# Four plain output row tiles become two, with tables shared by three head pairs and transposes taken half by half

## The chip, the cores and the metric

The kernel runs on one core of one Trainium2 chip. The metric is device time of one execution in microseconds. Engines are called TensorE (PE in the profile, its weight loads PEld), VectorE (DVE), ScalarE (ACT), GpSimd (POOL) and SyncE (SP), whose queue issues nearly all DMA transfers.

## What is computed

One layer: RMS norm of x (2048 rows of 1024), one projection to q, k, v and a gate, neighbourhood attention on a grid of 32 x 64 tokens with 16 heads of 64, a gate by SiLU, the output projection, the residual, and a last RMS norm.

```python
h = rmsnorm(x, norm_0)
q, k, v, gate = split(h @ w_in, 4)            # each (2048, 1024), 16 heads
# token (r, c) attends to 8 rows x 16 columns around it, clipped at the edges of the grid
s = q @ k.T / 8 + rpb[head, row offset, column offset]
o = softmax(s) @ v
x = x + (o * silu(gate)) @ w_out
return rmsnorm(x, norm_f)
```

All is float32. A float32 product is made as three matmuls of split operands: each operand is split into a high part (a ScalarE copy) and the rest (a VectorE subtraction), and high x high, high x low and low x high are summed in PSUM.

## The kernel before

**Products.** A product of a 2 x 2 block matrix is made by seven block products instead of eight ("seven products", Winograd's form). The input projection is made so in stages one and two, but for three units of it (`halves`, L252 on, 288 matmuls of 128x512) that are left for the time of attention. The output projection has 16 row tiles of 128 rows. Row tiles 0 to 3 (`PLAIN = 4`, L33) are plain: 24 matmuls for each half of the columns, 48 a tile (`outputs`, L1550). The others go in pairs by seven products of 12 matmuls each, 84 a pair, behind attention (`rows_by_seven`, L1708; `PAIRS`, L1601).

**Attention** is 32 runs (`order`, L1214): a run is a head pair p (0 to 7) and a row block T (0 to 3). First come T = 1 and 0 of all head pairs, then T = 2 and 3. A run has two quads of 32 query columns each. One pass of the main loop (L1811) works on two runs at once; in the order of TensorE's instructions it is

1. the filling: a given number of plain matmuls (`amount[m]`, L1753), first the 288 of the projection, then the plain row tiles. Between them lie the scaling of the second quad's softmax weights for run m-1 (`normalise`, L1330: GpSimd, ScalarE and VectorE a part each) and one or two operations that split weights or row tiles (`consume`, `split_rows`),
2. `turns(m - 1)` (L1347): 48 transposes of the softmax weights X, 16 for each of three PSUM bank pairs `ph`, each pair copied to `pta` by ScalarE and VectorE,
3. `scores(2m)` and `scores(2m+1)` (L1298): 64 matmuls s; VectorE adds the bias table and takes the maximum (L1320), ScalarE the exponential (L1327). They write X, so they come after the transposes that read it,
4. `values(m - 1)` (L1371): 36 matmuls o, one VectorE product with the gate, and the store of the result to `ogd[T]` in DRAM.

The amounts are 13.5 matmuls in every run but the first two and the last. A run wants its k (`load_k`), q, values, gate and bias table (`load_bias`, L1260) loaded; the loads are put into SyncE's queue at due times counted in filling matmuls (`begin`, L1790; `later_loads`, L1782): gate 1, bias 3 and 4.5, values 4, q 7, k 12. What isn't due at the end of a run is issued at the start of the next. A table is one of three kinds: "mid", "top" (brought by T = 0) and "end" (brought by T = 3). The middle table of a head pair is loaded for T = 1 and again for T = 2.

**Row tiles.** `load_og` (L1414) loads the gated result of a row tile from `ogd[T]`, `split_og` (L1424) splits it, `load_res` (L1420) loads the residual x into one of three buffers, which the square of the row (L1463) frees; `add_rows` and `finish` (L1436, L1471) add, square, take the root, scale and store. The order of the plain half tiles is `turns_` (L1532). Row pairs load their parts with `load_rows_of` (L1637).

Of the kernel before, what the change touches and what calls it, by code (L numbers as in the profile page):

```python
# [11 lines left out]
F32 = mybir.dt.float32  # L12
# [12 lines left out]
NP = H // 2  # L25
# [4 lines left out]
NF_SCALE = -2 * ROOT[0] * 0.375 * ROOT_K ** 2  # L30
NEG = -1e30
RES_BUFS, RES_EARLY = 3, 1
PLAIN = 4  # L33

FRAME, TALL = [0, 4, 12, 17], 15
HALF_ROWS = [[(0, 8), (0, 11)], [(0, 11), (4, 11)], [(0, 11), (4, 11)], [(3, 11), (7, 8)]]
# [25 lines left out]
def build(ctx, tc, x, xr, xt, wg, bias, w_out, n0, nf, out):  # L62
    nc = tc.nc
# [3 lines left out]
    kd = [dram.tile([128, S], F32, name=f"kd{p}") for p in range(NP)]  # L67
    sgd = [dram.tile([128, S], F32, name=f"sgd{p}") for p in range(NP)]
    vd = [dram.tile([4, S, 128], F32, name=f"vd{u}") for u in range(2)]
    ogd = [dram.tile([128, 4, NP, 128], F32, name=f"ogd{T}") for T in range(4)]  # L70
    vsd = {f: dram.tile([4, 128, 512], F32, name=f"vsd{f}") for f in ("S1", "S4")}
    vsp = {f: dram.tile([4, 2, 128, 512], F32, name=f"vsp{f}") for f in ("S2", "S3")}
    vu1 = dram.tile([4, 128, 512], F32, name="vu1")
# [9 lines left out]
    raw = pool("raw", 6)  # L83
# [36 lines left out]
    def bank(n, name):  # L120
        return banks.tile([128, n], F32, name=name, tag="bank")
# [208 lines left out]
    def store(key, lag, f):  # L330
        n = len(later)
        while n and later[n - 1][0] > clock[0] + lag:
            n -= 1
        later.insert(n, (clock[0] + lag, key, f))
# [856 lines left out]
    def projections():  # L1191
        for n, (kind, j, ph, c) in enumerate(halves):
            state["half"] = n
            w = (KINDS[kind] + j, ph)
            for a in range(2):
                if n == len(halves) - 5 and a == 0:
                    for k in range(RES_EARLY):
                        load_res(*turns_[k])
                if n == len(halves) - 1:
                    if a == 0:  # L1200
                        store(("ogl",), 20, lambda: (load_og(0), load_og(1)))
                    else:
                        store(("og0",), 19, lambda: split_og(0))
                consume(1)
                p = yield from group(w, a, c, n)
                state["event"] = clock[0]
                give(kind, 2 * j + a, c, p, True)
            state["done_halves"] = n + 1
# [2 lines left out]

    KT, VT, QT, EM, SG = {}, {}, {}, {}, {}
    stored_at = {}
    order = [(p, T) for p in range(NP) for T in (1, 0)] + [(p, T) for p in range(NP - 2) for T in (2, 3)]  # L1214
    order += [(NP - 2, 2), (NP - 1, 2), (NP - 1, 3), (NP - 2, 3)]
    pairs = [(p, T, quad) for p, T in order for quad in range(2)]
    PARTS = {1: (4, 19, 8), 0: (0, 4, 0), 2: (12, 28, 0), 3: (28, 32, 0)}
# [1 line left out]
    def load_k(p, T):  # L1219
        r0, r1, more = PARTS[T]  # L1220
        base = 12 * (T > 1)
        a, b = r0 * GW, r1 * GW + more
        must(*[("k", p, c) for c in range(a // 512, (b + 511) // 512)])

        def keys():
            if T in (1, 2):
                khalf.clear()
                KT[p, T // 2] = (kp([128, 2048], F32, "kt") if p % 2 == 0 else mkp([128, 1536], F32, "kt"))[:, :1344]
            t = KT[p, T // 2]
            if T == 2:  # L1230
                nc.gpsimd.memset(t[:, 1280:1288], 0.0)
            nc.sync.dma_start(t[:, a - base * GW:b - base * GW], kd[p][:, a:b])

        return keys
# [22 lines left out]
    kinds_of = {0: ("top", "mid"), 1: ("mid", "mid"), 2: ("mid", "mid"), 3: ("mid", "end")}  # L1257
    BRINGS = {0: "top", 1: "mid", 2: "mid", 3: "end"}

    def load_bias(p, T):  # L1260
        fs = []
        kind = BRINGS[T]
        w = 2 * WIDE * TABLES[kind][2]
        EM[p, T // 2, kind] = []
        for quad in range(2):
            t = mp([128, 512], F32, "em")[:, :w]
            EM[p, T // 2, kind].append([t[:, :w // 2], t[:, w // 2:]])
            o = TABLE_AT[kind] + quad * w
            fs.append(lambda t=t, o=o, w=w: nc.sync.dma_start(t, bias[p, :, o:o + w]))
        return fs  # L1270
# [27 lines left out]
    def scores(i, between=None):  # L1298
        p, T, quad = pairs[i]
        kt, qt = KT[p, T // 2], QT[p, T]  # L1300
        both = [bank(512, f"s{s}") for s in range(2)]
        places = {}
        for half, (u, n) in enumerate(HALF_ROWS[T]):
            for s in range(2):
                places[half, s] = both[s][:, 256 * half:256 * half + WIDE * n]
            for h in range(4):
                g = 4 * quad + h
                for s in range(2):
                    a = slice(s * 64, s * 64 + 64)
                    o = (FRAME[T] + u - 12 * (T > 1)) * GW + 8 * FIRST[g]  # L1310
                    nc.tensor.matmul(places[half, s][h * 32:h * 32 + 32], qt[a, g * 64 + half * 32:g * 64 + half * 32 + 32],  # L1311
                                     kt[a, o:o + n * GW].rearrange("p (r c) -> p r c", c=GW)[:, :, :WIDE],
                                     start=True, stop=True, skip_group_check=True)
        ST[i] = st = tiny.tile([128, 12], F32, name="st")
        for half, (u, n) in enumerate(HALF_ROWS[T]):
            xs_ = [by_column(X[quad, half, s], HALF_ROWS[T][half]) for s in range(2)]
            table = EM[p, T // 2, kinds_of[T][half]][quad]
            for s in range(2):
                o = 2 * half + s
                nc.vector.tensor_tensor_reduce(xs_[s], places[half, s].rearrange("p (r c) -> p c r", c=WIDE),  # L1320
                                               table[s].rearrange("p (c r) -> p c r", c=WIDE), -1.0, 1e38,
                                               OP.add, OP.min, st[:, o:o + 1])
            if between and half == 0:
                between()
            for s in range(2):
                o = 2 * half + s
                nc.scalar.activation(xs_[s], xs_[s], AF.Exp, bias=st[:, o:o + 1], scale=-1.0,  # L1327
                                     accum_out=st[:, 4 + o:5 + o])
# [18 lines left out]
    def turns(m):  # L1347
        p, T = order[m]
        k = 8 * TALL
        PT[m] = pt([128, 3072], F32, "pta")  # L1350
        t = PT[m].rearrange("p (s b n c) -> p b s n c", s=2, b=3, c=64)
        for b in range(3):
            ph = [bank(512, f"ph{h}") for h in range(2)]
            at = (2 - b) * k
            for quad in range(2):
                for half in range(2):
                    for s in range(2):
                        for h in range(2):
                            q = slice(64 * h, 64 * h + 64)
                            o = s * 256 + half * 128 + quad * 64  # L1360
                            nc.tensor.transpose(ph[h][:k, o:o + 64], X[quad, half, s][q, at:at + k], ident[q, q])  # L1361
            for h in range(2):
                o, i_ = t[:k, b, :, h::2], ph[h][:k].rearrange("p (s n c) -> p s n c", s=2, c=64)
                if h:
                    nc.vector.tensor_copy(o, i_)  # L1365
                else:
                    nc.scalar.activation(o, i_, AF.Copy)  # L1367
        if m + 1 < cycles:
            clear_x(order[m + 1][1])

    def values(m):  # L1371
# [16 lines left out]
        nc.vector.tensor_tensor(og, o, SG.pop((p, T)), OP.mult)  # L1388

        def keep():  # L1390
            nc.sync.dma_start(ogd[T][:, :, p], og.rearrange("p (i q) -> p i q", i=4))
            written.add(("og", p, T))
            stored_at[p, T] = clock[0]

# [19 lines left out]
    def load_og(n):  # L1414
        T, i = divmod(n, 4)
        must(*[("og", p, T) for p in range(NP)])
        G[n] = t = wp([128, NK, 128], F32, "ograw")
        nc.sync.dma_start(t, ogd[T][:, i])

    def load_res(n, j):  # L1420
        RES[n, j] = rbp([128, 512], F32, "xr")
# [14 lines left out]
    def add_rows(n, j, ps):  # L1436
        xr = RES.pop((n, j))
        state["event"] = clock[0]
        if n not in Y:
            Y[n] = [None, None], tiny.tile([128, 8], F32, name="st3")  # L1440
        y, st = (raw if j and n < 1 else ev)([128, 512], F32, "y"), Y[n][1]
        Y[n][0][j] = y
        if n == tiles - 1:
            cut = [slice(0, 256), slice(256, 512)] if j else [slice(0, 512)]
# [84 lines left out]
            scale()  # L1529
            store(("y", n), 18, send)  # L1530

    turns_ = [(0, 0), (1, 0), (2, 0), (0, 1), (1, 1), (2, 1), (3, 0), (3, 1)]  # L1532
    place = {}
    for k, (n, j) in enumerate(turns_):
        place.setdefault(n, k)
# [101 lines left out]
    def load_rows_of(m, f, home=None):  # L1637
        n, half = PAIRS[m][int(f[1]) - 1], int(f[2]) - 1
        T, i = divmod(n, 4)
        must(*[("og", p, T) for p in range(NP) if p // 4 == half])  # L1640
        A[m, f] = (home or raw)([128, 512], F32, "raw")
        nc.sync.dma_start(A[m, f].rearrange("p (k q) -> p k q", k=4), ogd[T][:, i, 4 * half:4 * half + 4])

    def form_rows(m, P):
        src = A[m, uses[P][0]]
# [103 lines left out]
                        f(*a)  # L1749

    cycles = len(order)
    dense, end_of_it = 13.5, 24
    amount = [dense] * 25  # L1753
    first = 16
    amount[0] -= first / 2
    amount[1] += first
    calm_debt = 3
    HEAD = 5
    amount += [(96 * (12 - len(units_two)) + 48 * PLAIN - sum(amount) - first - end_of_it) / (cycles - 25)] * (cycles - 25) + [end_of_it - 6]
    fill = projections()  # L1760
    outs = outputs()
    credit = [0.0]
# [19 lines left out]
    def later_loads(fs, lag, step):  # L1782
        for k, f in enumerate(fs):
            store(("load",), lag + k * step, f)
# [5 lines left out]
    def begin(m):  # L1790
# [11 lines left out]
        if m + 1 < cycles:  # L1802
            nx = order[m + 1]
            later_loads([load_q(*nx), load_k(*nx)], 7, 5)
            later_loads(load_bias(*nx), 3, 1.5)

    stage_one()
    stage_two()
# [92 lines left out]
```

## Time and profile before

| What | us |
| --- | --- |
| median of 3 runs | 990.86 (990.8 to 992.84) |
| the profiled execution | 991.77 |
| its span | 989.8 |
| attention, first scores to last o | 562.5 to 869.1 |
| row pairs by seven products | 869.15 to 983.6 |

All rows of the profile come from the one profiled execution. A run of attention is told by its transposes (L1361), of which the profile has 32 groups of 48.

### The profile page before, as it was taken

To read this page: it belongs to the slowest core of one execution; us is meant where nothing else is said; L and a number is where in the kernel's file an instruction comes from. 1 tells how busy PE (TensorE), PEld (TensorE's weight loads), DVE (VectorE), ACT (ScalarE), POOL (GpSimd) and SP (SyncE) were. 2 spreads that over 40 slices of the span, in tenths; PEclk is the share of its full clock that TensorE was granted. 3 is DMA by queue.
4 is the path that set the end of the run, shared out by engine and by line. 5 is a ranking of instruction groups with operands and counts; after the bars stand their busy time and mean duration, and the time that the engine had idled before them with its cause. 6 is when DMAs were issued, how large, how long until landed. Compare 5 with 4: busy or idle time off the path is not lost.

```text
span 989.8 us, 22264 instructions
## 1 busy us (share of the span) xinstructions
PE 979.6 (99%) x8172; PEld 797.4 (81%) x8172; DVE 757.3 (77%) x1703; ACT 532.5 (54%) x1310; POOL 148.1 (15%) x396
## 2 busy tenths in 40 slices
PE   9999999999999999999999999999999999999997
PEld 7888888888788888888888777778778777888886
DVE  5899888988565876766776577778878878877866
ACT  7773245465435342333433377677778776653443
POOL 0000001232100000000000033333333332311110
PEclk9999999999999999999999999999999999999999
DMA  8943547777957936657455899988999988997754
GB/s 287 334 131 104 197 130 251 250 224 253 350 179 216 293 117 183 206 165 241 166 184 188 229 275 278 270 260 265 296 287 294 286 227 265 304 369 188 204 148 117
DMA packets 149228, 227.89 MB, mean 230 GB/s; under 512 B 13312, under 2 KB 65792, under 8 KB 149120
## 3 DMA queue, kind: packets, MB, share of 16 engines
q1 hardware_dynamic: 146096, 221.37, 71.0%
q0 software_dynamic: 2592, 4.72, 2.8%
q8 instruction: 64, 1.05, 0.4%
q10 hardware_dynamic: 432, 0.40, 0.1%
q14 instruction: 44, 0.36, 0.1%
HBM read 160.37 MB, written 66.06 MB: 229 GB/s over the span
## 4 chain that ended last, share of the span: by engine, by line
PE 95%; DMA 3%; ACT 1%; DVE 1%; issue 0%; SPq 0%; ACTq 0%
PE pp L440 40%; PE pv L606 13%; PE py L1681 12%; PE o L1384 7%; PE s L1311 5%; PE ph L1361 4%; PE pv L721 2%; PE pp L384 2%; PE pp L388 2%; PE pp L386 2%; DMA kt<-kd 2%; PE po L1586 1%; PE po L1590 1%; PE po L1588 1%; DMA xr<-in_x_dram 1%; ACT x L1327 1%
## 5 line engine op out<-in xcount | busy, mean ns | idle before, releaser
L440 PE MATMUL pp<-h,f 128*128 128x512 f32 x576 | 185.3, 389 | 0.0
L440 PE MATMUL pp<-t,f 128*128 128x512 f32 x702 | 171.4, 389 | 0.0
L440 PEld LDWEIGHTS pp<-t,f 128*128 128x128 f32 x702 | 131.7, 188 | 27.6 <-DVE u L453 0.2
L1327 ACT ACTIVATE x<-x,st 128x253 f32<-128x253 f32 (+1 forms) x256 | 125.1, 496 | 32.9 <-DVE st L1320 32.9
L440 PEld LDWEIGHTS pp<-h,f 128*128 128x128 f32 x576 | 108.1, 188 | 22.6
L440 PE MATMUL pp<-l,f 128*128 128x512 f32 x288 | 112.1, 389 | 0.0
L1343 POOL TENSOR_SCALAR x<-x,st 128x253 f32<-128x253 f32 (+1 forms) x160 | 78.5, 510 | 130.5 <-DVE st L1332 127.1
L1320 DVE CUSTOM_DVE_ANT_0 x<-s,em 128x253 f32<-128x253 f32 (+1 forms) x256 | 87.3, 398 | 6.6 <-issue 4.5
L423 DVE TENSOR_TENSOR f<-raw,f 128x512 fp32r<-128x512 f32 x105 | 75.8, 727 | 20.0 <-ACT f L422 19.9
L1384 PEld LDWEIGHTS o<-pta,vt 120*64 120x64 f32 x1152 | 70.0, 137 | 18.4 <-issue 12.0
L1384 PE MATMUL o<-pta,vt 120*64 120x192 f32 (+2 forms) x1152 | 84.1, 299 | 0.0
L422 ACT ACTIVATE f<-raw 128x512 fp32r<-128x512 f32 x105 | 63.7, 623 | 36.2 <-DVE raw L429 22.0
L1365 DVE COPY pta<-ph 120x512 f32<-120x512 f32 x96 | 60.3, 684 | 13.6 <-PE ph L1361 13.1
L1367 ACT ACTIVATE pta<-ph 120x512 f32<-120x512 f32 x96 | 50.5, 599 | 33.8 <-PE ph L1361 33.6
L440 PEld LDWEIGHTS pp<-l,f 128*128 128x128 f32 x288 | 54.1, 188 | 11.2
L1681 PE MATMUL py<-woh,f 128*128 128x512 f32 x192 | 60.9, 390 | 0.0
L1311 PE MATMUL s<-kt,q 64*32 64x253 f32 (+1 forms) x2048 | 58.7, 362 | 2.2 <-DMA kt<-kd 1.7
L1361 PEld LDWEIGHTS ph<-ident,x 64*120 64x120 f32 x1536 | 47.6, 135 | 11.3 <-issue 10.6
L606 PE MATMUL pv<-wh,t 128*128 128x512 f32 x176 | 56.4, 390 | 0.1
L440 PE MATMUL pp<-sixths,f 128*128 128x512 f32 x198 | 52.7, 389 | 0.0
L461 POOL TENSOR_TENSOR tmp<-tmp,rb 128x512 f32<-128x512 f32 x18 | 28.4, 1580 | 158.0 <-DVE tmp L458 138.3
L1361 PE MATMUL ph<-ident,x 64*120 64x64 f32 x1536 | 52.0, 221 | 0.0
(230 smaller groups left out, 1883.7 us busy)
## 6 DMA issues: line engine op xcount, KB each, us to landing
raw<-in_wg_dram SPq DMA_DIRECT2D x124, 256.0 KB
vt<-vd SPq DMA_DIRECT2D x32, 480.0 KB
row<-in_xr_dram SPq DMA_DIRECT2D x32, 256.0 KB
vd<-v SPq DMA_DIRECT2D x32, 256.0 KB
sgd<-sg SPq DMA_DIRECT2D x32, 256.0 KB
q<-qd SPq DMA_DIRECT2D x32, 256.0 KB
sgt<-sgd SPq DMA_DIRECT2D x32, 256.0 KB
ogd<-og SPq DMA_DIRECT2D x32, 256.0 KB
```

Source lines behind the costliest of these rows:

```text
L422: nc.scalar.activation(t[:, 0], src, AF.Copy)
L423: nc.vector.tensor_tensor(t[:, 1], src, t[:, 0].bitcast(F32), OP.subtract)
L440: nc.tensor.matmul(B[n, P], t[:, int(m == 2), c], x[k][int(m == 1)], start=P in (1, 6, 5) and k == 0 and m == 0, stop=k == 3 and m == 2, s ...
L606: nc.tensor.matmul(p, a[:, o], b, start=P in (1, 6, 5) and k == 0 and m == 0, stop=k == 3 and m == 2, skip_group_check=True)
L1311: nc.tensor.matmul(places[half, s][h * 32:h * 32 + 32], qt[a, g * 64 + half * 32:g * 64 + half * 32 + 32], kt[a, o:o + n * GW].rearrange(" ...
L1320: nc.vector.tensor_tensor_reduce(xs_[s], places[half, s].rearrange("p (r c) -> p c r", c=WIDE), table[s].rearrange("p (c r) -> p c r", c=W ...
L1327: nc.scalar.activation(xs_[s], xs_[s], AF.Exp, bias=st[:, o:o + 1], scale=-1.0, accum_out=st[:, 4 + o:5 + o])
L1343: nc.gpsimd.tensor_scalar(t, t, st[:, o:o + 1], 1.0, op0=OP.mult, op1=OP.mult)
L1361: nc.tensor.transpose(ph[h][:k, o:o + 64], X[quad, half, s][q, at:at + k], ident[q, q])
L1365: nc.vector.tensor_copy(o, i_)
L1384: nc.tensor.matmul(o[s * 64:s * 64 + 64, g0 * 64:g1 * 64], vt[:k, strip, s * 64:s * 64 + 64], moving, start=strip == 0, stop=strip == 7, s ...
L1681: nc.tensor.matmul(B[m, P], t[:, a, c], b, start=P in (1, 6, 5) and k == 0 and i == 0, stop=k == 3 and i == 2, skip_group_check=True)
```

## The change

- `PLAIN` 4 to 2: row tiles 0 and 1 are plain (96 matmuls of filling), tiles 2 to 15 go in seven pairs by seven products (six before). The y tile of the first row comes from the pool `ev` and not from `raw`.
- The amounts of filling become 10.0 for 23 runs (with the same shift in the first two) and (384 - 238 - 16 - 24) / 9 = 11.8 for the next.
- Head pairs 0 to 2 (`SHARED = 3`) run T = 1, 0, 2, 3 one behind the other and share one middle table: T = 2 loads none. At their T = 2 the first middle table of the next head pair is asked for two runs ahead.
- The buffers of k alternate by the count of loads, not by the head pair.
- `turns`: the transposes go in six blocks of eight, (bank pair, quad) = (0,0), (1,0), (0,1), (2,0), (1,1), (2,1); a bank pair is copied after its second block.
- `ogd` is laid out [128, 8, 4, 128] and not [128, 4, 8, 128]: a store writes 2 KB in one piece for each partition (4 x 512 B before), a load of a row tile or of half a row tile reads pieces of 512 B (4 KB and 2 KB before).
- The loads of the first two row tiles are due 24 and not 20 matmuls into the last half.

```diff
-PLAIN = 4
+PLAIN = 2
+SHARED = 3
...
-    ogd = [dram.tile([128, 4, NP, 128], F32, name=f"ogd{T}") for T in range(4)]
+    ogd = [dram.tile([128, NP, 4, 128], F32, name=f"ogd{T}") for T in range(4)]
...
-                        store(("ogl",), 20, lambda: (load_og(0), load_og(1)))
+                        store(("ogl",), 24, lambda: (load_og(0), load_og(1)))
...
-    order = [(p, T) for p in range(NP) for T in (1, 0)] + [(p, T) for p in range(NP - 2) for T in (2, 3)]
+    order = [(p, T) for p in range(SHARED) for T in (1, 0, 2, 3)]
+    order += [(p, T) for p in range(SHARED, NP) for T in (1, 0)] + [(p, T) for p in range(SHARED, NP - 2) for T in (2, 3)]
...
-                KT[p, T // 2] = (kp([128, 2048], F32, "kt") if p % 2 == 0 else mkp([128, 1536], F32, "kt"))[:, :1344]
+                KT[p, T // 2] = (mkp([128, 1536], F32, "kt") if len(KT) % 2 else kp([128, 2048], F32, "kt"))[:, :1344]
...
-    def load_bias(p, T):
+    def table_at(p, T, kind):
+        return p, 0 if p < SHARED else T // 2, kind
+
+    def load_bias(p, T, upto=2):
...
-        EM[p, T // 2, kind] = []
-        for quad in range(2):
+        got = EM.setdefault(table_at(p, T, kind), [])
+        for quad in range(len(got), upto):
...
-            table = EM[p, T // 2, kinds_of[T][half]][quad]
+            table = EM[table_at(p, T, kinds_of[T][half])][quad]
...
-        for b in range(3):
-            ph = [bank(512, f"ph{h}") for h in range(2)]
+        ph = {}
+        for b, quad in ((0, 0), (1, 0), (0, 1), (2, 0), (1, 1), (2, 1)):
+            if quad == 0:
+                ph[b] = [bank(512, f"ph{h}") for h in range(2)]
             at = (2 - b) * k
-            for quad in range(2):
-                for half in range(2):
-                    for s in range(2):
-                        for h in range(2):
+            for half in range(2):
+                for s in range(2):
+                    for h in range(2):
...
+            if quad == 0:
+                continue
             for h in range(2):
...
-            nc.sync.dma_start(ogd[T][:, :, p], og.rearrange("p (i q) -> p i q", i=4))
+            nc.sync.dma_start(ogd[T][:, p], og.rearrange("p (i q) -> p i q", i=4))
...
-        nc.sync.dma_start(t, ogd[T][:, i])
+        nc.sync.dma_start(t, ogd[T][:, :, i])
...
-        y, st = (raw if j and n < 1 else ev)([128, 512], F32, "y"), Y[n][1]
+        y, st = ev([128, 512], F32, "y"), Y[n][1]
...
-    turns_ = [(0, 0), (1, 0), (2, 0), (0, 1), (1, 1), (2, 1), (3, 0), (3, 1)]
+    turns_ = [(0, 0), (1, 0), (0, 1), (1, 1)]
...
-        nc.sync.dma_start(A[m, f].rearrange("p (k q) -> p k q", k=4), ogd[T][:, i, 4 * half:4 * half + 4])
+        nc.sync.dma_start(A[m, f].rearrange("p (k q) -> p k q", k=4), ogd[T][:, 4 * half:4 * half + 4, i])
...
-    dense, end_of_it = 13.5, 24
-    amount = [dense] * 25
+    dense, end_of_it = 10.0, 24
+    many = 23
+    amount = [dense] * many
...
+            if order[m][0] < SHARED and order[m][1] == 2:
+                later_loads(load_bias(*order[m + 2], 1), 6, 0)
```

## What I predict

> **What bounds the kernel now.** I read the page first, then the chain of waits, then the timeline of two runs (a run is one pass of the attention loop: one head pair on one row block T), then windows.
>
> ```profile
> span 989.8 us, 22264 instructions
> PE 979.6 (99%) x8172; PEld 797.4 (81%) x8172; DVE 757.3 (77%) x1703; ACT 532.5 (54%) x1310; POOL 148.1 (15%) x396
> PEclk9999999999999999999999999999999999999999
> PE 95%; DMA 3%; ACT 1%; DVE 1%; issue 0%; SPq 0%; ACTq 0%
> ```
>
> TensorE works 99% of the span, and 95% of the chain is its own work, so a matmul that goes saves its time, provided the others can keep up with a shorter run. In the chain of waits (start, length, what) a run of the attention loop looks like this; the last row is the row tiles by seven products.
>
> ```profile
> 649.17 1.56 PE ph L1361 x48
> 650.73 1.64 PE s L1311 x64
> 652.36 2.55 PE o L1384 x36
> 658.31 1.56 PE ph L1361 x48
> 659.87 1.87 PE s L1311 x64
> 667.46 1.56 PE ph L1361 x48
> 869.15 114.49 PE py L1681 x504
> ```
>
> Each run is 48 transposes (1.56 us), 64 score matmuls (1.64 narrow, at T = 0 and 3, or 1.87 wide, at T = 1 and 2), 36 value matmuls (2.55) and the filling, 13.5 plain matmuls on the mean. Two runs take 667.46 - 649.17 = 18.29 us, so 9.15 each. Behind attention a matmul costs 114.49 / 504 = 0.227 us, without a break.
>
> What has to be ready at the transposes is read from the timeline of a wide run, followed by a narrow one (start, length, engine, line, what).
>
> ```profile
> 677.28 1.89 DVE L1365 COPY pta<-ph 120x512 f32<-120x512 f32 x3 [0.43 <-PE ph L1361]
> 683.63 1.26 POOL L1343 TENSOR_SCALAR x<-x,st 128x253 f32<-128x253 f32 x2
> 684.18 0.85 DVE L1339 TENSOR_SCALAR x<-x,st 128x253 f32<-128x253 f32 x2
> 685.26 1.30 DVE L191 TENSOR_TENSOR wol<-raw,woh 128x512 fp32r<-128x512 f32 x2 [0.22 <-ACT woh L190]
> 685.67 1.63 PE L1361 MATMUL ph<-ident,x 64*120 64x64 f32 x48
> 686.47 1.88 DVE L1365 COPY pta<-ph 120x512 f32<-120x512 f32 x3
> 692.87 0.80 DVE L1339 TENSOR_SCALAR x<-x,st 128x253 f32<-128x253 f32 x2
> 694.01 1.29 DVE L191 TENSOR_TENSOR wol<-raw,woh 128x512 fp32r<-128x512 f32 x2 [0.33 <-ACT woh L190]
> 694.81 1.63 PE L1361 MATMUL ph<-ident,x 64*120 64x64 f32 x48
> ```
>
> Follow VectorE from copies to copies. Its three copies of transposed weights start 677.28; the softmax weights of the second quad are scaled at 684.18 + 0.85 = 685.03 (GpSimd's share at 684.89), 7.75 us after the copies began; TensorE comes to the transposes at 685.67. So a wide run has 0.64 us to spare, a narrow one 694.81 - 693.67 = 1.14. Between the scaling and the next copies lie the splittings of weights (L191), 0.69 us each. With two of them the wide run's next copies begin 686.47, right as they end: VectorE's line has no slack there already.
>
> **The change part by part.** Fillings leave attention: 96 plain matmuls go, 84 come behind it.
>
> ```profile
> 655.18 0.39 PE L386 MATMUL pp<-l,w 128*128 128x512 f32 x1
> 657.92 0.39 PE L386 MATMUL pp<-l,w 128*128 128x512 f32 x1
> 866.00:990.00 124.00, 117.63 (x543) 96.90 (x541) 91.11 (x177) 52.29 (x123) 15.93 (x18) 0.99 0.70 205
> ```
>
> These two fillings are twelve apart, (657.92 - 655.18) / 12 = 0.228 us. So attention loses 96 x 0.228 = 21.9 us and the end gains 84 x 0.227 = 19.1: **-2.8 us**, if the shorter runs hold. In the window behind attention VectorE works 91 of 124 us and DMA 0.70, so the seventh pair's splittings, sums and transfers lie beside TensorE; I take 0 for them, bounds 0 and 1 us (one late operand).
>
> A run in the first 23 now has ten fillings. From 9.15 us the wide one loses three (8.46), the narrow one four (8.23); two make 16.69.
>
> The half-by-half order. Six blocks of eight transposes, 1.56 / 6 = 0.26 us each: two of the first quad come first, so the second quad is needed 0.52 us later than the transposes start. Against that a bank is full only after three blocks, not two, so the copies begin 0.26 us later. Net 0.26 us to the good. The spare of a wide run becomes 0.64 - 0.69 - 0.26 + 0.52 = 0.21, of a narrow one 1.14 - 0.91 + 0.26 = 0.49. Both are positive, so a run without other work stays TensorE's.
>
> Now the work in between. What the run may take, copies to copies, is 8.46 wide and 8.23 narrow. What VectorE needs: with one splitting, 685.95 - 677.28 = 8.67 wide and 694.70 - 686.47 = 8.23 narrow (0.69 us after the start of each L191 row); with both, 9.19 (the start of the next copies) and 694.01 + 1.29 - 686.47 = 8.83. A wide and a narrow run with one each need 16.90 against 16.69, 0.2 us too much; with two each 18.02, 1.3 us too much. The numbers of these splittings, from the groups of lines inside attention (575 to 866):
>
> ```profile
> L191 DVE TENSOR_TENSOR wol<-raw,woh 128x512 fp32r<-128x512 f32 x16 | 10.5, 689 | 2.7 <-ACT woh L190 2.7
> L186 DVE TENSOR_TENSOR w<-raw,w 128x512 fp32r<-128x512 f32 x8 | 5.5, 692 | 1.8 <-ACT w L185 1.8
> L1431 DVE TENSOR_TENSOR gl<-ograw,gh 128x512 fp32r<-128x512 f32 x8 | 5.2, 686 | 1.6 <-ACT gh L1430 1.6
> ```
>
> The eight of L186 fall one to a run in the first six or so: three pairs at 0.2, 0.6 us. The first eight of L191 fall into some five runs of ten fillings, 1.6 a run, some 0.9 a pair: two pairs, 1.8 us (the runs around them have spare for the rest). The last eight and the two row tiles' L1431 (four operations now, not eight) fall into runs of 11.8 fillings, 0.8 us a pair longer: 0.4. Together **+2.8 us**. The bounds are 0 (all of it taken up by runs with spare) and each of the 28 operations 0.2 us too long, 5.6 (those in twos cost more, single ones in narrow runs nothing).
>
> Waits of before that may go. Two places of the chain are longer than a run; below them are two rows of SyncE's queue from the timeline, and one of its waits (total, times, longest):
>
> ```profile
> 731.46 1.60 PE ph L1361 x48
> 742.07 1.54 PE ph L1361 x48
> 797.39 1.17 PE ph L1361 x35
> 799.73 9.36 DMA kt<-kd
> 817.13 1.60 PE ph L1361 x48
> 789.47 0.32 SPq L1255 DMA_DIRECT2D sgt<-sgd  x1
> 796.32 0.33 SPq L1422 DMA_DIRECT2D xr<-in_x_dram  x1
> SPq L1422 <- ACT xr L1463: 6.7, 2, 6.2
> ```
>
> 742.07 - 731.46 = 10.61, so 1.46 lost; 817.13 - 797.39 = 19.74 for two runs, 1.45 lost. The second begins on SyncE's queue: a load of the residual x (L1422) stood from 789.8 to 796.3 for the square that frees its buffer, and the bias, q and k loads queued behind it came late. Eight such loads become four, for three buffers, so one can still wait where five could. I take **-1.4 us** for it and leave the other place, the first row tile's splitting, which only moves; bounds -2.9 and 0.
>
> DMA. The loads per run stay, the run shrinks.
>
> ```profile
> 575.00:866.00 291.00, 288.43 (x5065) 229.74 (x5064) 232.94 (x821) 216.65 (x683) 96.29 (x340) 1.00 0.91 276
> 690.00:727.00 37.00, 37.00 (x653) 29.55 (x651) 29.45 (x103) 28.30 (x89) 12.68 (x46) 1.00 0.93 295
> em<-in_bias_dram SPq DMA_DIRECT2D x32, 253.0 KB
> ogd<-og SPq DMA_DIRECT2D x32, 256.0 KB
> ```
>
> Attention moves 291 x 276 GB/s = 80 MB at a share of 0.91. Shared tables take six loads of 253 KB away (1.6 MB), two row tiles less some 3 MB (their products, residuals and results, 512 KB each): 75.6 MB in about 270 us, 280 GB/s, a share of 0.92. But head pairs 3 to 7 on T = 1 and 0, where nothing is shared, go from 0.93 to 0.93 x 9.15 / 8.35 = 1.02, less the projections' stores that come rarer: some 1.0. A k load that is late there cost 1.45 us. I take half of one, **+0.8**, bounds 0 and three, 4.4. The k load is due after 12 fillings and a run has ten, so it goes out at the start of the next run; on SyncE's queue it still stands behind q and ahead of the next gate load, so nothing new comes in front of it. The first tables of the next pair come two runs early into a buffer of their own, which waits for nobody.
>
> At nothing: the products' layout (256 KB stores in pieces of 2 KB instead of 512 B, loads the other way round) is hidden by the next run's work, and at the end by the DMA share of 0.70; uncovered, one load of 256 KB at 276 GB/s would be 0.9 us. The y tile's other buffer and the alternation of k buffers issue nothing.
>
> Sum: -2.8 + 2.8 - 1.4 + 0.8 = **-0.6 us**. The profiled execution took 991.77 us, 2.0 of them around the span; it stands 0.9 above the median 990.86. So 991.2 by its own time, and **990.3** as a median.
>
> [...] The granted clock is 1.00 in every window above, with its 10.6 us run and all its transposes. [...]
>
> **The rivals.** *The spare is enough* (0.35): the runs without splittings take up the rest and DMA keeps up; -2.8 - 1.4 and 0.4 of remainders, 987.0. For it: positive spares of 0.21 and 0.49. Against it: the two-splitting run at 686.47. *VectorE's line becomes the bound* (0.15, slower): decides from two splittings in a wide run on, or if the second quad's scaling misses 0.21 us of spare in every wide run; +5.6 instead of +2.8 and the xr wait back, 994.4. *Transfers* (0.09): at a share of 1.0 three or four k loads late at 1.45 us each, 990.3 - 0.8 + 5 = 994.5. *The halves do not take hold* (0.03): a bank or the second quad still holds the first block, 0.52 us in each of 16 wide runs less their spare, (0.52 - 0.21) x 16 = 5 us, 995. [...]
>
> **How the numbers follow.** My forecast has 0.37, with a range of its own of 988.9 to 992.8, that is within 0.2%, about what a measurement of this kernel can tell from no change. Faster is the first rival, 0.35; slower are the four others, 0.28. The range from 986.5 to 995.5 takes in the first rival and the price of each bound alone; both bounds together, and the clock, stay outside.
>
> **What would show it.** Right: distances of transposes of 8.2 to 8.5 us in runs without splittings, about 16.7 a pair; the row tiles' chain 588 x 0.227 = 133.6 us; copies that begin 1.0 us after the transposes; no xr wait of 6 us on SyncE. Wrong: idle time of PE's loads released by the scaling (L1339, L1343) in most wide runs; k loads in the chain more than once; a granted clock under 1; or runs with splittings no longer than those without.

## The result and the profile after

The changed kernel takes **1008.6 us** (median of 4 runs, 1005.34 to 1012.18) where the kernel before took 991.85 beside it (4 runs). The estimated ratio is 1.0153, with a 95% interval of 1.0125 to 1.0181: slower by 1.5%, far outside the predicted range (the quotient of the two medians is 1.0169). The profiled execution took 1009.55 us, 17.8 more than that of before. Its page:

```profile
span 1007.6 us, 22323 instructions
PE 982.4 (97%) x8160; PEld 800.7 (79%) x8160; DVE 757.3 (75%) x1702; ACT 534.7 (53%) x1317; POOL 152.6 (15%) x399
...
PE 76%; DMA 11%; DVE 5%; ACT 4%; issue 3%; SPq 1%; POOL 1%; DVEq 0%; POOLq 0%; ACTq 0%
```

TensorE has 12 matmuls fewer but is idle for 25.2 us of the span (1007.6 - 982.4) where it was idle for 10.2. Its own work fell from 95% to 76% of the chain that ended last, and transfers rose from 3% to 11%.

Where the time lies is seen from the first transposes of the first and of the last run of attention. A group of 48 starts at the first of the two times (the columns: shortest, median and longest matmul in ns, then the first and the last start); first the kernel before, then after:

```profile
L1361 PE MATMUL ph<-ident,x x48: 217/218/268, 575.8 to 577.2; 64*120 64x64 f32 x48
L1361 PE MATMUL ph<-ident,x x48: 217/218/268, 863.8 to 865.3; 64*120 64x64 f32 x48
```

```profile
L1367 PE MATMUL ph<-ident,x x48: 217/218/269, 573.1 to 575.2; 64*120 64x64 f32 x48
L1367 PE MATMUL ph<-ident,x x48: 217/218/268, 862.2 to 863.6; 64*120 64x64 f32 x48
```

Up to the first transposes the changed kernel gains 575.8 - 573.1 = 2.7 us, since some fillings lay there. The 31 runs between took 288.0 us and take **289.1**. From the last transposes to the end it loses 145.4 - 126.0 = 19.4, the 84 matmuls that were to be added (84 x 0.227 = 19.1). So the second half of the exchange happened as worked out and the first did not: 87 fillings have gone from those 31 runs, 87 x 0.228 = 19.8 us, and the runs are no shorter. What TensorE waits for (total, times, longest), over the whole span, the costliest first:

```profile
PE s L1316 <- DMA kt<-kd: 11.3, 7, 4.1
PE o L1392 <- issue: 3.1, 2, 1.8
PE s L1316 <- ACT pta L1375: 2.1, 2, 1.8
```

In the kernel before the first of these rows is `1.7, 2, 1.4` and the other two don't exist. The scores wait for k in seven runs of 31. An eighth wait, of 1.84 us at 729.09, is put down to ScalarE's copies in the third row, but these had ended at 728.15; its k load went out late too (724.27), so it is probably k's as well. The transfers themselves aren't denser: the window that holds both attentions (busy time of each engine, granted clock, DMA share, GB/s), first after, then before:

```profile
576.00:862.00 286.00, 269.19 (x4873) 215.80 (x4873) 215.58 (x778) 208.49 (x665) 96.17 (x330) 0.99 0.88 260
```

```profile
576.00:862.00 286.00, 283.43 (x5003) 225.87 (x4999) 229.17 (x815) 213.88 (x678) 95.81 (x339) 1.00 0.91 276
```

0.88 against 0.91. Runs that wait for nothing are as short as predicted. Here are two, from TensorE's part of the timeline, with VectorE's copies of the transposed weights:

```profile
671.93 1.62 PE L1367 MATMUL ph<-ident,x 64*120 64x64 f32 x48
680.48 1.63 PE L1367 MATMUL ph<-ident,x 64*120 64x64 f32 x48
688.76 0.68 PE L1367 MATMUL ph<-ident,x 64*120 64x64 f32 x16
672.92 1.89 DVE L1373 COPY pta<-ph 120x512 f32<-120x512 f32 x3 [1.13 <-PE ph L1367]
```

Distances 8.55 and 8.28 (8.46 and 8.23 were predicted), copies 0.99 us behind the transposes (1.0 predicted).

The longest run shows what happens to k. SyncE's queue in order, from the timeline, then the chain (start, length, what):

```profile
731.11 0.33 SPq L1234 DMA_DIRECT2D kt<-kd  x1
...
737.82 0.42 SPq L1399 DMA_DIRECT2D ogd<-og  x1
...
739.62 0.49 SPq L1243 DMA_DIRECT2D q<-qd  x1
740.15 0.44 SPq L374 DMA_DIRECT2D qd<-q  x1
744.17 0.32 SPq L1399 DMA_DIRECT2D ogd<-og  x1
744.54 0.43 SPq L1234 DMA_DIRECT2D kt<-kd  x1
```

```profile
743.53 0.63 DVE og L1396
...
744.17 0.32 SPq L1399
...
744.54 6.87 DMA kt<-kd
...
751.54 3.15 PE s L1316 x64
```

The load of k (L1234) at 731.11 was ahead of the store of its run's result (L1399, 737.82). The next one was not: behind the q load stands the store, which waits until VectorE's product (L1396) is done at 744.16, and only then does k go, 744.54. Its transfer takes 6.87 us and the scores start at 751.54 instead of about 747.5, 4.1 us late. In SyncE's timeline only one other k load stands so, behind a second store: that of 724.27, for the scores at 729.09. The other six late loads follow q as they did in the kernel before. The run from 745.84 to 760.08 is 14.24 us long where an undisturbed one has 8.5 at most.

### The profile page after: what moved, and what is told of

It is laid out like the page before. It is cut to its first block, busy times and chain, and to the rows that moved or that the text cites. A ratio compares the mean times of both kernels' runs of the same rounds, so it can differ in the third digit from the quotient of the medians.

```text
span 1007.6 us, 22323 instructions
## 1 busy us (share of the span) xinstructions
PE 982.4 (97%) x8160; PEld 800.7 (79%) x8160; DVE 757.3 (75%) x1702; ACT 534.7 (53%) x1317; POOL 152.6 (15%) x399
## 4 chain that ended last, share of the span: by engine, by line
PE 76%; DMA 11%; DVE 5%; ACT 4%; issue 3%; SPq 1%; POOL 1%; DVEq 0%; POOLq 0%; ACTq 0%
PE pp L441 29%; PE py L1689 13%; PE pv L607 13%; PE o L1392 5%; DMA kt<-kd 5%; PE s L1316 4%; PE ph L1367 3%; PE pv L722 2%; ACT x L1332 2%; DMA raw<-in_w_out_dram 2%; DMA raw<-in_wg_dram 1%; PE pp L387 1%; PE pp L385 1%; PE pp L389 1%; DVE vs L662 1%
## 5 line engine op out<-in xcount | busy, mean ns | idle before, releaser
L424 DVE TENSOR_TENSOR f<-raw,f 128x512 fp32r<-128x512 f32 x105 | 75.9, 727 | 19.5 <-ACT f L423 19.4
L1316 PE MATMUL s<-kt,q 64*32 64x253 f32 (+1 forms) x2048 | 62.5, 368 | 13.7 <-DMA kt<-kd 11.3
L1689 PE MATMUL py<-woh,f 128*128 128x512 f32 x224 | 71.3, 390 | 0.0
L441 PEld LDWEIGHTS pp<-l,f 128*128 128x128 f32 x288 | 54.0, 188 | 11.3
L1316 PEld LDWEIGHTS s<-kt,q 64*32 64x32 f32 x2048 | 42.8, 107 | 21.7 <-issue 8.3
```

The source lines that it names most:

```text
L424: nc.vector.tensor_tensor(t[:, 1], src, t[:, 0].bitcast(F32), OP.subtract)
L441: nc.tensor.matmul(B[n, P], t[:, int(m == 2), c], x[k][int(m == 1)], start=P in (1, 6, 5) and k == 0 and m == 0, stop=k == 3 and m == 2, s ...
L1689: nc.tensor.matmul(B[m, P], t[:, a, c], b, start=P in (1, 6, 5) and k == 0 and i == 0, stop=k == 3 and i == 2, skip_group_check=True)
```

## The experiments

Eleven kernels ran in three sets, each beside its own runs of the kernel before (medians 993.44, 994.05 and 993.39 us). Ratios are estimates against these runs; they can differ from the quotient of the medians by up to 0.2%. Where a time of attention is given, it is from profiled executions.

**1 to 4: which part?** The first set takes the wait for k, the number of transfers and the block order apart.

The queue's place alone, in the changed kernel. q and k are asked for 1 and 2 fillings into a run instead of 7 and 12:

```diff
-            later_loads([load_q(*nx), load_k(*nx)], 7, 5)
+            later_loads([load_q(*nx), load_k(*nx)], 1, 1)
```

> The changed kernel, with the loads of q and k due 1 and 2 fillings into a run instead of 7 and 12, so ahead of the store of the attention result, of the values and of the second bias table. Theory Q (the loads of k come late because of their place in SyncE's queue, behind a store that waits for VectorE): the seven waits of the scores for k, 11.3 us, go, and the time falls to 995 to 999. Theory B (the transfers as a whole do not fit into the shorter run): the waits only move to other loads, under 4 us gained. Theory V (VectorE's line): no change beyond 1 us.

Measured 997.5 us (10 runs, 992.02 to 1001.41), ratio 1.0039 [1.0012, 1.0066]: three quarters of the loss have gone (from 1.5% to 0.4%). No wait of the scores for k is left in the list of waits. In the timeline of SyncE's queue and the chain of this kernel:

```profile
741.63 1.02 SPq L1243 DMA_DIRECT2D q<-qd  x1
742.71 0.65 SPq L1234 DMA_DIRECT2D kt<-kd  x1
...
743.93 0.38 SPq L1399 DMA_DIRECT2D ogd<-og  x1
```

```profile
755.28 1.92 PE s L1316 x64
```

q and k now stand ahead of the store (743.93), and k is asked for 755.28 - 742.71 = 12.6 us before its scores. For the run that waited longest it is 14.2 us (724.20 to 738.41); in the changed kernel that was 751.54 - 744.54 = 7.0, with a transfer of 6.9. The window shows that the transfers had room, at a higher share than with the late loads:

```profile
576.00:862.00 286.00, 284.94 (x5013) 228.95 (x5012) 227.91 (x810) 215.66 (x679) 96.58 (x334) 1.00 0.91 277
```

The number of transfers alone: all head pairs use the bias tables of the first one, so the other tables aren't loaded (52 loads fewer).

```diff
     def table_at(p, T, kind):
-        return p, 0 if p < SHARED else T // 2, kind
+        return 0, 0, kind
...
             if order[m][0] < SHARED and order[m][1] == 2:
-                later_loads(load_bias(*order[m + 2], 1), 6, 0)
+                pass
```

> The changed kernel, but every head pair takes the bias tables of the first: six tables are loaded and stay, 52 loads of 184 or 253 KB (some 11 of 80 MB in attention) go. Part of the computation is changed by it. Theory B: run lengths fall to 8.3 and 8.5 us nearly throughout, 990 to 994. Theory Q: two loads fewer stand in front of q and k, but k stays behind the store, some 3 to 6 us gained. Theory V: no change.

Measured 1010.7 us (4 runs), ratio 1.0170 [1.0104, 1.0237]: as slow as with all tables, as far as four runs with this spread (1003.9 to 1015.95) can tell. The DMA share falls to 0.77, and the scores still wait for k:

```profile
576.00:862.00 286.00, 274.52 (x4941) 218.39 (x4938) 217.31 (x782) 211.15 (x671) 97.01 (x338) 0.99 0.77 223
```

```profile
PE s L1316 <- DMA kt<-kd: 6.0, 3, 3.1
```

So the amount that is moved isn't all of it, but it has a part: the waits for k fall from 11.3 us to 6.0. Of these, 2.36 are at 729.12 and 3.09 at 748.95, the two runs whose k load stands behind a second store; of the others only 0.5 us is left. The expectation of a gain fails even so. This profile has 4.0 us of TensorE's stops without a wait, and a clock of 0.51 behind one of them (last section), which may hide it.

The block order of the transposes: the changed kernel with both quads of a bank one after the other, as before.

```diff
-        for b, quad in ((0, 0), (1, 0), (0, 1), (2, 0), (1, 1), (2, 1)):
+        for b, quad in ((0, 0), (0, 1), (1, 0), (1, 1), (2, 0), (2, 1)):
```

> The changed kernel with the transposes in the order of before (both quads of a bank pair, then the next pair). By the sum of the prediction wide runs miss 0.05 us of spare each and runs with splittings 0.26 us: 2 to 5 us slower. Theories Q and B: the waits for loads take up that loss, so 0 to 2 us slower.

Measured 1008.36 us (4 runs), ratio 1.0150 [1.0107, 1.0193]: no difference. Late loads could hide one, so it is tried again in experiment 11.

The other way round: the kernel before with the block order and the layout of the products of the change, and nothing else.

```diff
-    ogd = [dram.tile([128, 4, NP, 128], F32, name=f"ogd{T}") for T in range(4)]
+    ogd = [dram.tile([128, NP, 4, 128], F32, name=f"ogd{T}") for T in range(4)]
...
-            for quad in range(2):
+        for b, quad in ((0, 0), (1, 0), (0, 1), (2, 0), (1, 1), (2, 1)):
```

> The kernel before with the half-by-half order of transposes and the new layout of the products alone, its fillings at 13.5. All theories: TensorE is the bound there and spares are 0.6 and 1.1 us, so within 1 us of the kernel before; if the layout or the order itself costs, 3 us or more slower.

Measured 994.92 us (10 runs), ratio 1.0017 [0.9987, 1.0046]: these two parts make no difference that can be measured.

**5 to 8: the place in the queue, in both kernels.** In the changed kernel k is asked for after 9 fillings, within most runs, but later than q:

```diff
-            later_loads([load_q(*nx), load_k(*nx)], 7, 5)
+            later_loads([load_q(*nx), load_k(*nx)], 7, 2)
```

> The changed kernel with the load of k due after 9 fillings, not 12, and q left at 7. In SyncE's queue this takes two loads of k (head pairs 6 and 7 at T = 1) from behind the store of the next run to before it; the others stay behind q. If the store is what delays k where a run had only 7 fillings, the two waits of 1.84 and 4.09 us at 729 and 751.5 go and the others stay: 5 to 8 us less than the changed kernel, 1000 to 1004. If the place behind this run's own store, values and table matters too, the rest of the 11 us needs q and k early.

Measured 1003.55 us (4 runs), ratio 1.0099 [1.0072, 1.0125]: about a third of the loss has gone. No k load stands behind a second store any more, and the wait of 1.84 us at 729 is gone. That of 4.1 us is not: the same run, whose scores now start at 747.42, still waits 3.56 us. In SyncE's timeline two loads of w_out hold the queue from 729.00 to 735.40 there, k goes out at 738.25, 5.6 us before TensorE is ready, and takes 9.04 us. With the others it is 8.7 us in 7 waits. So the second store is one thing that costs; too short a lead, whatever holds the queue, is the other.

The early place in the kernel before, the same edit as experiment 1:

> The kernel before with q and k due 1 and 2 fillings into a run. Its scores waited 1.7 us for k in two places; these go, and nothing else changes since its runs are TensorE's: 1 to 2 us faster than the kernel before. If early q and k push values or tables too late, slower.

Measured **989.93 us** (8 runs, 987.84 to 993.05), ratio 0.9965 [0.9946, 0.9984]: faster than both kernels, by more than expected. Its page:

```profile
span 986.1 us, 22290 instructions
PE 98%; ACT 1%; DMA 0%; DVE 0%; issue 0%; ACTq 0%
```

And the reverse: the kernel before, with all its fillings and transfers, but k due after 18 fillings, so that it falls into the next run, behind that run's store.

```diff
-            later_loads([load_q(*nx), load_k(*nx)], 7, 5)
+            later_loads([load_q(*nx), load_k(*nx)], 7, 11)
```

> The kernel before with the load of k due after 18 fillings, 4.5 into the next run, so that most of its loads stand behind that run's store, which waits for VectorE's product (some 6.6 us after the transposes). The loads then go out some 4 to 7 us before the scores want them, and take 6 to 7 us: theory Q gives 1 to 4 us of waiting in most of 30 runs, 1020 to 1080, at full filling and the same transfers. Theories B and V: no change.

Measured 1029.82 us (4 runs), ratio 1.0364 [1.0328, 1.0399]. Runs of full length, none of the change in them, and yet more than twice the loss. Half of the k loads (15 of 32) then stand behind a second store:

```profile
PE s L1311 <- DMA kt<-kd: 26.6, 16, 4.1
```

The place of one load in a queue is enough by itself. By its due time alone it would go out only 1.5 fillings later, 0.34 us, since what isn't due at the end of a run is issued at the start of the next; the rest is what stands ahead of it.

The last of this set asks what is left in experiment 1. It has the early loads, and the subtraction that splits the output weights goes from VectorE to GpSimd:

```diff
             nc.scalar.activation(h, t, AF.Copy)
-            nc.vector.tensor_tensor(l, t, h.bitcast(F32), OP.subtract)
+            nc.gpsimd.tensor_tensor(l, t, h.bitcast(F32), OP.subtract)
```

> The changed kernel with q and k early as before, and the subtraction that splits w_out (16 times 0.69 us on VectorE) made on GpSimd instead. If VectorE's line is what is left of the lost time (runs 13, 16, 18, 23 to 29 are 0.2 to 2.4 us longer than 8.28 and 8.52), 2 to 4 us less than with q and k early alone, 991 to 995; if GpSimd's longer subtraction holds up its scaling of the softmax weights, no gain or a loss.

Measured 996.08 us (10 runs), ratio 1.0013 [0.9988, 1.0038], against 1.0039 [1.0012, 1.0066]: the intervals overlap and the sets differ, so the gain isn't shown by the times (the profile of this run has 4.5 us of the stops of the last section, which could hide one). What it takes away is seen in a run of experiment 1 with two splittings (L192) ahead of the copies:

```profile
710.65 1.76 PE L1367 MATMUL ph<-ident,x 64*120 64x64 f32 x48
711.58 1.29 DVE L192 TENSOR_TENSOR wol<-raw,woh 128x512 fp32r<-128x512 f32 x2 [0.22 <-ACT woh L191]
712.79 1.88 DVE L1373 COPY pta<-ph 120x512 f32<-120x512 f32 x3
```

The copies come 712.79 - 710.65 = 2.14 us behind the transposes instead of 0.99, and the run takes 9.52 us where an undisturbed narrow one with its 13 fillings would take 8.28 + 3 x 0.228 = 8.96.

**9 to 11: the shorter filling alone.** The kernel before, its order of runs, tables, block order and layout untouched, with nothing but the filling of the change (the y tile's buffer and the due time of the first row tiles' loads go with it and aren't printed):

```diff
-PLAIN = 4
+PLAIN = 2
...
-    turns_ = [(0, 0), (1, 0), (2, 0), (0, 1), (1, 1), (2, 1), (3, 0), (3, 1)]
+    turns_ = [(0, 0), (1, 0), (0, 1), (1, 1)]
...
-    dense, end_of_it = 13.5, 24
-    amount = [dense] * 25
+    dense, end_of_it = 10.0, 24
+    amount = [dense] * 23
```

> The kernel before with nothing but the shorter filling: two more row tiles by seven products behind attention, ten fillings in the first 23 runs; order of the runs, bias tables, transposes and layout as before. Theory F (the fewer fillings make the q and k loads late, and nothing else in the change matters): 1003 to 1013 us, a ratio of 1.012 to 1.02, with waits of the scores for k of 8 us or more in attention. Rival G (the new order of the head pairs or the shared tables bring a good part of the loss): under 998 us. Rival H (the other parts earned something that the change needs): over 1016 us, with transposes that wait for the second quad in most wide runs.

Measured 1010.76 us (4 runs), ratio 1.0159 [1.0117, 1.0200]: the whole loss, with the same wait to a few tenths.

```profile
PE s L1311 <- DMA kt<-kd: 11.5, 7, 4.2
```

The new order of the head pairs and the shared tables are thereby cleared too. The same with the early loads of experiment 1:

> The same shorter filling in the kernel before, with the q and k loads asked for one filling into the run, ahead of the store of the result. Theory F: as the changed kernel with early loads, 993 to 1000 us, a ratio of 1.000 to 1.008, with no wait for k over 0.5 us. What is then left over the kernel before with early loads (989.9) is VectorE's line, 4 to 8 us. If the halves, tables and order earn something on a short run, it is over 1000.

Measured 995.09 us (10 runs), ratio 1.0015 [0.9997, 1.0032]; no wait for k is left. Once the value matmuls wait for their values, 2.4 us.

Last, experiment 1 with the old block order, where no late load covers a difference:

> The changed kernel with early q and k loads and the transposes in the old order of blocks (both quads of a bank at once), now without late loads to hide a difference. By the prediction's sum each wide run then lacks 0.52 - 0.21 = 0.31 us, 16 x 0.31 = 5 us over the changed kernel with early loads (997.5): 1002 us. Rival: the block order makes no difference, within 2 us of 997.5, runs still 8.5 and 8.3 us apart.

Measured 993.8 us (10 runs), ratio 1.0003 [0.9991, 1.0015]; the rival holds, and the loss of 5 us that the prediction's sum would give isn't there. Its undisturbed runs:

```profile
660.76 1.63 PE L1367 MATMUL ph<-ident,x 64*120 64x64 f32 x48
669.00 1.63 PE L1367 MATMUL ph<-ident,x 64*120 64x64 f32 x48
677.46 1.63 PE L1367 MATMUL ph<-ident,x 64*120 64x64 f32 x48
```

8.24 and 8.46 us, 0.04 to 0.09 shorter than with the halves (8.28 and 8.55 above). Whether it is faster than experiment 1 stays open: they ran in different sets, and the intervals overlap.

## Why the prediction was wrong

**The step that failed** is in its part on DMA: "on SyncE's queue it still stands behind q and ahead of the next gate load, so nothing new comes in front of it", and with it the term of +0.8 us, bounds 0 to 4.4. It looked at the neighbours of k in one list of due times, left out what else goes through the same queue, and took half of one late load where seven came, probably eight. Two things were missed.

First, the store of a run's result goes through this queue too, due after 4 fillings of the next run, and it waits there for VectorE's product; what has not gone before it waits with it. A run doesn't have ten fillings each time: two have 7 (a bigger neighbour is paid back), as the one just ahead of the transposes at 735.35. The store is then due after 7 + 4 = 11 fillings and k after 12, so k goes behind the store. That is so for two loads, and the sentence is wrong for these alone. The rows at 740.15 to 744.54 show the longer one, and experiment 7 shows what it costs when half of the loads stand so: 3.6% of the time.

Second, due times counted in fillings are times counted in matmuls, not in us of lead: the load's issue (0.43 us in the median in both kernels) and its transfer (6.7 and 9.4 us for the two in the chain of the kernel before) didn't shrink with the run, while the run lost 0.6 to 0.9 us. For the other six late loads the sentence holds, k follows q, and they are late all the same, by 7.2 us together; in the chain five of them take 7.0 to 10.1 us from issue to landing. Experiment 5 shows that taking away the first alone doesn't do, experiment 2 that the second goes nearly away with fewer transfers, and experiment 1 that a longer lead takes away both.

What it cost: 11.3 us of waits for k against 1.7, and with what comes along 17.3 us, the difference of the 31 runs of attention between the changed kernel (289.1) and experiment 1, from its rows:

```profile
L1367 PE MATMUL ph<-ident,x x48: 217/218/268, 573.6 to 575.7; 64*120 64x64 f32 x48
L1367 PE MATMUL ph<-ident,x x48: 217/218/268, 845.4 to 846.8; 64*120 64x64 f32 x48
```

845.4 - 573.6 = 271.8. Of the 17.3 us, 11.3 are the waits for k in the list, 1.8 the wait at 729.09, and 1.7 matmuls at a lower clock behind the longest wait (scores 3.15 us for 1.92, values 2.98 for 2.55). Another 2.8 are stops of TensorE without a wait (3.1 us against 0.3), and no run shows that these have to do with k. All this is from single executions, and that of experiment 1 (993.43) is 4.1 us faster than its median; by the ratios, 1.0153 and 1.0039, the late loads cost 1.1%, some 11 us.

The rival "Transfers" named the right victim, three or four late k loads at 1.45 us, which is near the 7.2 us of the six. Its reason, a DMA share near 1.0, isn't seen in the mean, which fell to 0.88. But traffic has a part, as experiment 2 shows; what the rival lacks is the store.

**Fillings, -2.8: right in both halves.** 87 of the 96 gone between the first and last transposes are 19.8 us, nine lay ahead; behind attention 84 x 0.227 = 19.1 were due and 19.4 came. The tail is 588 row matmuls in one piece of work:

```profile
867.74 54.64 PE py L1689 x240
922.41 79.14 PE py L1689 x348
```

54.64 + 79.14 = 133.8, predicted 133.6. VectorE's work and the seventh pair's transfers did lie beside them.

**VectorE, +2.8 (bounds 0 to 5.6): right in kind, too small.** Experiment 1 against experiment 6 has no late loads on either side. There 271.8 stands against 285.5 us:

```profile
L1361 PE MATMUL ph<-ident,x x48: 217/218/268, 574.7 to 576.1; 64*120 64x64 f32 x48
L1361 PE MATMUL ph<-ident,x x48: 217/218/268, 860.2 to 861.6; 64*120 64x64 f32 x48
```

13.7 gained where 87 fillings make 19.8; 6.1 us are given back. Some 1.5 of these are the undisturbed run itself, longer by about 0.05 us with the halves (31 x 0.05; experiments 4 and 11 show it too); it shows in the scores, here of a wide and a narrow run of experiment 1, which take 1.87 and 1.64 in the kernel before:

```profile
738.48 1.92 PE s L1316 x64
...
747.01 1.68 PE s L1316 x64
```

The rest, about 4.6, lies in five runs, those that begin at 574, 684, 711, 728 and 789 us, 0.6 to 1.5 us each over an undisturbed run with as many fillings. All have splittings, or the scaling of the gate, ahead of the copies or of the second quad's scaling. That this is VectorE's line is read from the timeline; that moving work off it helps was not clear in the times (experiment 8). The prediction worked with two runs that it had looked at; the first run, where three splittings fall together, and the gate were in none of its terms.

**The halves, 0.26 us a run to the good: wrong.** Experiments 3, 4 and 11 show no gain. The rival that priced their failure at 5 us was wrong as well, by the same sum: it counted the 0.52 us for which the second quad is needed later and forgot that the copies then also begin 0.26 later, and that the old order needs the second quad only after its first block. The old order's spare is 0.64 - 0.69 + 0.26 = 0.21 us, the same as with the halves. The sign that the prediction set against itself did appear: TensorE's weight loads wait for the scaling of the second quad in 15 groups of transposes (5.3 us in sum, 0.4 at most; 0.7 us in two in the kernel before). The transposes themselves wait for it only once, 0.2 us, so this costs little.

**The wait for the residual on SyncE, -1.4: not gained in the changed kernel.** Two waits became one, but the long one, 6.2 us, is still there with 5.7 (SyncE's waits from 560 to 880 us, the kernel after):

```profile
SPq L1430 <- ACT xr L1471: 5.7, 1, 5.7
```

It ends at 823.86; the queue then issues without a pause up to the k load at 827.10, and the scores of that run are 1.60 us late. With early loads (experiment 1) the wait is still there, 3.4 us, but no k load is late behind it.

**The clock, 0.01: a consequence, not a cause.** On the mean it is 0.99 in attention, but behind the longest wait it is far lower. (The prediction read 1.00 in every window; its window behind attention has 0.99, which changes nothing.) The windows behind a wait of 2.1 us (739.15) and behind that of 4.1 (751.54) in the changed kernel:

```profile
739.10:741.00 1.90, 1.85 (x68) 1.43 (x70) 0.93 (x6) 0.31 (x1) 0.00 (x0) 1.00 0.94 338
751.50:754.70 3.20, 3.16 (x66) 1.99 (x68) 1.45 (x8) 1.11 (x5) 0.00 (x0) 0.60 1.07 246
```

After 4.1 us of waiting the clock was granted at 0.60, and the 64 scores took 3.15 us where the other wide runs have 1.92: 1.2 us on top of the wait. The length of the wait alone doesn't decide it: one of 3.56 us in experiment 5 left the clock at 1.00, and one of 1.79 us in experiment 7 was followed by 0.50 (last section). What decides it, no run shows. No run shows the term that the prediction has for a drop of the clock, 0.01 of its 0.28 for slower (0.28 - 0.15 - 0.09 - 0.03): the windows of the kernel before have 0.99 and 1.00. In its place the runs showed lower clocks behind waits for k, 0.60 here (1.7 us of longer matmuls) and 0.50 in experiments 2 (3.09 us, at 748.95) and 7 (1.79 us), and 0.51 behind a stop (last section).

**The table loads, the layout and the y tile's buffer, 0**: experiments 2, 4 and 9 show nothing against it.

**The sum as measured**, over the 31 runs between the two groups of transposes: from 288.0 us, 2.5 are the waits of the kernel before (285.5 in experiment 6), 19.8 go with the fillings, 6.1 are given back by VectorE and the halves, and 17.3 go with the late loads and the stops: 288.0 - 2.5 - 19.8 + 6.1 + 17.3 = 289.1. With 2.7 gained ahead and 19.4 paid behind, the span is 17.8 us longer. Without late loads on either side 986.1 becomes 991.7 (the spans of experiments 6 and 1; the ratios are 0.9965 and 1.0039, and 1.0003 in experiment 11): even with the loads in their right place the shorter filling gives back more than the twelve matmuls save. These are again single executions; by the ratios some 8 us are given back, not 6.1, and the late loads cost some 11.

## What to carry to other kernels

On SyncE's queue here k stood behind a store that waited until 744.16 and went out only at 744.54, and with 15 of 32 loads placed so the time was 3.6% longer (experiment 7): before work is made shorter, list what stands in that queue over two turns of the loop, stores included, and put loads that only need a free buffer ahead of stores that wait for results. Due times that are counted in the work to be removed move with it, while the transfers of k were no shorter here (6.9 to 10.1 us in the chain, 6.7 and 9.4 before); count the lead in microseconds, and take the shortest turn, not the mean one. A kernel whose chain is 95% one engine's work can have no reserve at all: here the cheapest gain was in the kernel before, 0.35% for two numbers in one line.

## What was not expected of the hardware

- **Behind a wait of 1.79 us the clock was granted at 0.50.** This was a wait for k in experiment 7, while behind one of 2.06 us in the changed kernel the clock was 1.00 (windows of 2 us behind them, that of experiment 7 first):

```profile
657.10 0.92 PE L1361 MATMUL ph<-ident,x 64*120 64x64 f32 x25 [0.63 <-issue]
659.81 3.00 PE L1311 MATMUL s<-kt,q 64*32 64x184 f32 x64 [1.79 <-DMA kt<-kd]
```

```profile
659.81:661.81 2.00, 2.00 (x48) 1.49 (x56) 0.12 (x1) 0.00 (x0) 0.00 (x0) 0.50 0.77 199
739.15:741.15 2.00, 2.00 (x70) 1.55 (x72) 1.03 (x6) 0.46 (x3) 0.00 (x0) 1.00 0.94 339
```

  The narrow scores took 3.00 us instead of 1.64. Ahead of this wait stand 48 transposes, which began at 655.55 and were themselves broken by a stop of 0.63 us, so for 659.81 - 655.55 = 4.26 us TensorE made no matmuls but these. That these transposes have a part in it isn't shown: in experiment 2 a stop of 2.1 us ahead of a value matmul was followed by 0.51:

```profile
659.74:661.74 2.00, 2.00 (x7) 1.45 (x7) 1.24 (x4) 0.46 (x1) 0.40 (x1) 0.51 0.02 9
```

  So the cause stays open; no run took the transposes away from ahead of a wait.
- **TensorE stood still where the profile shows no wait.** In the changed kernel it stopped for 1.82 us at 658.95 and for 1.25 at 694.88, in the middle of the 36 value matmuls, where the profile shows nothing that it waits for. Such stops of 0.3 to 2.5 us are in all profiles with the shorter filling (4.0 us in experiment 2, 3.5 in 11, 0.3 in 1), and in one with the full filling, that of experiment 7; the kernel before, 4 and 6 have none. They don't go with the DMA share in attention, which is 0.77 in experiment 2, nor with late loads, which experiment 11 doesn't have. What they are stays open.
